# Layer 0 of the context tokens runs in front of the latent tokens, and one latent tile of layer 0 takes gathered experts

## The chip, the cores and the metric

The kernel runs on one core of one Trainium2 chip. The metric is the device time of one execution in microseconds (us): the median of three runs. The profile is one further execution, taken by the hardware profiler. The engines are TensorE (PE, with its weight loads listed as PEld), VectorE (DVE), ScalarE (ACT), GpSimd (POOL) and SyncE (SP). Each runs its own instruction queue in order; SP, ACT and POOL also issue DMA transfers from their queues.

## The reference, cut to what matters

Two layers act on 512 latent tokens x (four tiles of 128) beside 256 context tokens ctx (two tiles). Each layer is: norm, one input projection, differential attention, pooling, short convolution, gates, output projection; then norm and a PEER layer that picks 128 single-neuron experts for each token out of 16384.

```
for l in range(2):
    xn, cn = modulate(rms_norm(h)), modulate(rms_norm(hc))
    k, v of ctx come from cn; ctx attends to ctx alone, x attends to x and ctx
    mix   = mixer_output(attn, pool, conv, gates of xn) @ w_out     # x, both layers
    mix_c = the same of cn                                         # ctx, layer 0 only
    h  = h  + mod[2]  * mix;    h  = h  + mod[5]  * peer_ffn(norm(h))
    hc = hc + mod_c[2]* mix_c;  hc = hc + mod_c[5]* peer_ffn(norm(hc))   # layer 0 only
return h

def peer_ffn(xc):                       # per chunk of 128 tokens
    eidx, gate = product-key top 16 of each of 8 heads   # 128 experts for a token
    hid = gelu(einsum('td,thkd->thk', xc, u_emb[eidx]))
    return einsum('thk,thkd->td', gate * hid, v_emb[eidx])
```

In layer 1 the context gives only its k and v, and its own output is not needed. So the context's layer 0 result is needed late, by layer 1's attention, while x needs the context's layer 0 k and v early.

## The kernel before, in words

Activations lie transposed, channels on partitions and tokens in the free dimension. Every float32 product is made of three float32r matmuls (high times high, high times low, low times high): lines L98, L99 and L100 in `mm3`. A weight tile is loaded raw by SP, and `split` (L93 on ACT, L94 on DVE) makes its high and low half, so each 128x1024 piece costs one ACT and one DVE instruction.

The PEER layer has two forms. **Dense**: all 16384 experts are computed for the tile, and the gates of those not picked are zero. `hidden` runs 128 groups of 24 matmuls (`hid`), `values` 128 groups of 24 (`dps`), with the tokens of all dense tiles as columns: 512 columns for four tiles, 384 for three. `gates` writes the gate matrix, `weigh` multiplies it in. **Gathered**: in `gathered` each token of one tile fetches its own 128 rows of `peer_u` and 128 of `peer_v`; that is 256 indirect DMAs of 128x1024 floats for a tile, issued by POOL (L846) into a ring of three buffers named `row`. Each is consumed by one DVE instruction: L859 (a dot product, for `peer_u`) or L869 (a sum into `gacc`, for `peer_v`). The fetch of a row waits until the DVE instruction three rows back has freed its buffer.

Before, both context tiles of layer 0 and one x tile of layer 1 (`nd = XT - 1`) are gathered: 768 fetches. All four x tiles of layer 0 are dense. Layer 0 projects q, k and v for x and ctx together (`qkv`, one load of each weight for both), attends for both, runs the mixers of ctx and the pooling of x, then `ctx_ffn`, then the other mixers of x, and the x experts. The gathers of ctx are put 40000 behind in priority.

The order of each engine's queue is set when the kernel is built: a tile scheduler with a timeline (`schedule_with_timeline_sim`) places instructions by priority and by the times that it supposes. `prio(shift)` moves the priority of what is written inside. On the chip the queues run in that order whatever the real times are, so a late fetch holds everything that stands behind its consumer on DVE.

Of the kernel before, what the change touches and what calls it, by code (L numbers as in the profile page):

```python
# [21 lines left out]
F32 = mybir.dt.float32  # L22
# [47 lines left out]
class Net:  # L70
# [137 lines left out]
    def rotary(self, l, pool):  # L208
# [4 lines left out]
        nc.sync.dma_start(rows, bass.AP(tensor=r.tensor, offset=r.offset + 384 * l, ap=[[0, P], [1, 2 * HD]]))  # L213
        cs = pool.tile([P, XT, 2, 32], F32, name="cs")
# [10 lines left out]
        gains = [rows[:, off:off + HD] for off in (R_QG, R_KG)]  # L225
# [73 lines left out]
    def qkv(self, l, streams, kinds):  # L299

        nc, a = self.nc, self.a
        with ExitStack() as es:
            ap_ = self.pool(es, f"at{l}{streams[0].i}", 2)
            pm = self.pool(es, f"atm{l}{streams[0].i}", 3, PSUM)
            pt_ = self.pool(es, f"att{l}{streams[0].i}", 2, PSUM)
            rot = self.rotary(l, self.pool(es, f"rot{l}{streams[0].i}"))
# [88 lines left out]
    def attend(self, l, es, parts, side=None):  # L395

        nc = self.nc
        name = f"hd{l}"
# [3 lines left out]
        for s, k0, nk in parts:  # L402
            qs, ks = slice(s.o, s.o + s.n), slice(k0 * P, (k0 + nk) * P)
            for h in range(NH):
# [9 lines left out]
                self.head(l, ap_, pss, pt_, q, k, kl, v, h, s, nk)  # L414

    def head(self, l, ap_, pss, pt_, q, k, kl, v, h, s, nk):
        nc, nq = self.nc, s.nt
        A = []
        for qt in range(nq):
            qc = qt * P  # L420
            at = ap_.tile([P, nk * P], F32, tag="a", name="at", bufs=6)
# [173 lines left out]
    def conv_out(self, l, s, pp, z, m, gates):  # L595

        nc, a = self.nc, self.a
        with ExitStack() as es:
            zp = self.pool(es, f"co{l}{s.i}", 1)
            for c in range(4):  # L600
                g = gates[2 * c:2 * c + 2] if gates else self.conv_gate(l, s, pp, zp, c, 3)
                w = self.load_w(a["conv_out_w"][l, c], KT, 256)
                for cb in range(2):
                    j, t = 2 * c + cb, g[cb]
                    q = zp.tile([P, s.n], F32, tag="cq", name="cq", bufs=3)
                    nc.sync.dma_start(q, self.md[l][j * P:(j + 1) * P, s.o:s.o + s.n])
                    nc.vector.tensor_tensor(t, self.proj_t(pp, self.sub(w, cb), [z])[0][0], t, op=OP.mult)
                    nc.vector.tensor_tensor(t, t, q, op=OP.add)
                    self.split(m.h[:, j], m.l[:, j], t)
# [198 lines left out]
    def values(self, l, n, cs, W, pools, vq, acc, first, last=None):  # L808
# [3 lines left out]
        for dq in range(4):  # L812
# [9 lines left out]
            for db in range(2):  # L822
# [9 lines left out]
                if last is not None:  # L832
                    ht = last.tile([P, n], F32, name="fh", bufs=2)
                    nc.sync.dma_start(ht, self.hmid[l][j * P:(j + 1) * P, 0:n])
                    nc.vector.scalar_tensor_tensor(acc[:, j], acc[:, j], self.modT[l][:, 40 + j, 0:1], ht, op0=OP.mult, op1=OP.add)
                    dst = self.out if l == DEPTH - 1 else self.hout
                    nc.sync.dma_start(dst[j * P:(j + 1) * P, 0:n], acc[:, j])


    def gathered(self, l, tiles, gp, gq, nat, late):  # L840

        nc, a = self.nc, self.a

        def fetch(t, idx, s):
# [367 lines left out]
```

## Time and profile before

| what | us |
|---|---|
| median of three runs | 5145.29 |
| lowest and highest run | 5134.71 and 5170.3 |
| the profiled execution | 5138.01 |
| its span, first to last instruction | 5136.2 |
| PE busy in the span | 4934.7 (96%) |
| DVE busy | 3946.9 (77%) |
| POOL busy | 1180.5 (23%) |
| first matmul of x's dense layer 0 (`hid`) | at 1349.1 |
| first layer 1 matmul of x's norm | at 2986.8 |
| first matmul of the norm in front of layer 1's experts | at 3814.1 |

Matmuls overlap in the pipeline, and the duration of one is longer than its share of time. How fast PE really goes is read from how many matmuls start in a full 100 us, which the window rows below give behind "PE busy" as (x...). The same column of POOL counts the fetches where a window is cut to the tile `row`.

### The profile page before, as it was taken

The numbers are of one execution on the slowest core, as the hardware profiler recorded it, in microseconds if no ns is written. First come the engines' busy times: TensorE is split into PE (matmuls) and PEld (weight loads), VectorE is DVE, ScalarE is ACT, GpSimd is POOL, SyncE is SP. The second block draws the span as 40 slices with busy tenths as digits, with TensorE's granted clock in tenths as the row PEclk, the third lists the DMA queues.
The fourth block names the chain that finished last, engine by engine and source line by source line (L and its number), as shares of the span: only waits on it lengthen the run. The fifth ranks groups of instructions, "written<-read, shape, count | busy, mean of one in ns | idle before, by whom it ended". The sixth has DMA issues, their size and how long they took to land.

```text
span 5136.2 us, 73940 instructions
## 1 busy us (share of the span) xinstructions
PE 4934.7 (96%) x27373; PEld 4195.8 (82%) x27373; DVE 3946.9 (77%) x7993; ACT 1988.4 (39%) x2968; POOL 1180.5 (23%) x1028
## 2 busy tenths in 40 slices
PE   8999999998899999989999999999999999899999
PEld 5688787776688788768888789777679999899999
DVE  5457676697899998568888867666359999787885
ACT  4346664422333344222233234544334344332333
POOL 0001000024433343333333300000000434344320
PEclk9999999999999999999999999999999999999999
DMA  8667453468897889999999845533355888988995
GB/s 305 239 200 224 137 191 108 155 200 273 302 316 259 285 312 339 329 321 326 336 341 344 311 137 166 161 126 97 109 172 174 277 309 331 330 314 294 329 317 177
DMA packets 509035, 1280.77 MB, mean 249 GB/s; under 512 B 42496, under 2 KB 224640, under 8 KB 500352
## 3 DMA queue, kind: packets, MB, share of 16 engines
q1 hardware_dynamic: 302816, 669.35, 38.5%
q0 software_dynamic: 131968, 449.90, 25.7%
q10 hardware_dynamic: 73888, 156.79, 8.1%
q8 instruction: 215, 3.52, 0.3%
q14 instruction: 148, 1.21, 0.1%
HBM read 1098.13 MB, written 177.73 MB: 248 GB/s over the span
## 4 chain that ended last, share of the span: by engine, by line
PE 64%; DMA 14%; DVE 11%; issue 7%; POOL 2%; ACT 1%; SPq 0%; ACTq 0%; POOLq 0%; DVEq 0%
PE mm L98 6%; DMA row<-peer_v,ix 6%; PE mm L100 6%; PE mm L99 6%; DMA row<-peer_u,ix 6%; PE dps L99 5%; PE dps L100 5%; PE dps L98 5%; PE hid L100 4%; PE hid L98 4%; PE hid L99 4%; PE qk L98 3%; PE qk L100 3%; PE qk L99 2%; POOL row L846 2%
## 5 line engine op out<-in xcount | busy, mean ns | idle before, releaser
L100 PE MATMUL hid<-yh,ul 128*128 128x512 f32 (+1 forms) x2048 | 760.2, 372 | 33.9 <-DVE ul L94 33.6
L98 PE MATMUL hid<-yh,uh 128*128 128x512 f32 (+1 forms) x2048 | 757.1, 370 | 21.0 <-ACT yh L286 13.2
L846 POOL DMA_INDIRECT row<-peer_v,ix x384 | 568.5, 1480 | 876.7 <-DVE gacc L869 501.1
L846 POOL DMA_INDIRECT row<-peer_u,ix x384 | 521.4, 1358 | 1059.7 <-DVE row L859 617.7
L99 PE MATMUL hid<-yl,uh 128*128 128x512 f32 (+1 forms) x2048 | 755.7, 369 | 2.3 <-DVE yl L287 2.3
L98 PE MATMUL dps<-wh,vh 128*128 128x512 f32 (+1 forms) x2048 | 735.1, 365 | 20.0 <-ACT vh L93 18.6
L99 PE MATMUL dps<-wl,vh 128*128 128x512 f32 (+1 forms) x2048 | 741.7, 365 | 12.3 <-DVE wl L94 12.3
L100 PE MATMUL dps<-wh,vl 128*128 128x512 f32 (+1 forms) x2048 | 742.0, 364 | 10.4 <-DVE vl L94 10.4
L98 PE MATMUL mm<-hi,whi 128*128 128x512 f32 (+1 forms) x1856 | 666.5, 360 | 12.3 <-DVE y L582 3.1
L100 PE MATMUL mm<-hi,wlo 128*128 128x512 f32 (+1 forms) x1856 | 660.6, 358 | 14.0 <-DVE wlo L94 14.0
L99 PE MATMUL mm<-lo,whi 128*128 128x512 f32 (+1 forms) x1856 | 662.4, 357 | 3.5 <-DVE lo L94 3.5
L859 DVE SCALAR_TENSOR_TENSOR row<-row,gx 128x1024 f32<-128x1024 f32 x384 | 467.0, 1221 | 170.3 <-DMA row<-peer_u,ix 169.5
L869 DVE SCALAR_TENSOR_TENSOR gacc<-row,gw,gacc 128x1024 f32<-128x1024 f32 x381 | 488.1, 1281 | 133.7 <-DMA row<-peer_v,ix 132.6
L94 DVE TENSOR_TENSOR wlo<-wraw,whi 128x1024 fp32r<-128x1024 f32 (+1 forms) x356 | 427.2, 1202 | 179.6 <-ACT whi L93 177.2
L93 ACT ACTIVATE uh<-uraw 128x1024 fp32r<-128x1024 f32 x256 | 271.5, 1061 | 716.4 <-PE hid L99 651.9
L93 ACT ACTIVATE whi<-wraw 128x1024 fp32r<-128x1024 f32 (+1 forms) x356 | 370.5, 1043 | 404.4 <-PE mm L99 305.2
L93 ACT ACTIVATE vh<-vraw 128x1024 fp32r<-128x1024 f32 x256 | 270.2, 1058 | 641.9 <-PE dps L99 395.1
L100 PEld LDWEIGHTS hid<-yh,ul 128*128 128x128 f32 x2048 | 390.2, 191 | 82.9 <-DVE ul L94 44.6
L98 PEld LDWEIGHTS hid<-yh,uh 128*128 128x128 f32 x2048 | 391.1, 191 | 64.1 <-ACT yh L286 15.6
L98 PEld LDWEIGHTS dps<-wh,vh 128*128 128x128 f32 x2048 | 386.7, 189 | 61.9 <-ACT vh L93 19.4
L99 PEld LDWEIGHTS dps<-wl,vh 128*128 128x128 f32 x2048 | 387.1, 189 | 54.8 <-DVE wl L94 14.4
L100 PEld LDWEIGHTS dps<-wh,vl 128*128 128x128 f32 x2048 | 387.2, 189 | 51.5 <-DVE vl L94 11.1
(332 smaller groups left out, 9480.4 us busy)
## 6 DMA issues: line engine op xcount, KB each, us to landing
uraw<-uT SPq DMA_DIRECT2D x256, 512.0 KB, 5.7
vraw<-v SPq DMA_DIRECT2D x256, 512.0 KB, 6.8
wraw<-w_in SPq DMA_DIRECT2D x216, 512.0 KB, 4.4
gd<-gst ACTq DMA_DIRECT2D x28, 2048.0 KB, 10.7
mw<-w_mod SPq DMA_DIRECT2D x96, 512.0 KB, 7.0
wraw<-wq SPq DMA_DIRECT2D x80, 512.0 KB, 6.0
hidd<-ge ACTq DMA_DIRECT2D x128, 256.0 KB, 5.6
G<-gd SPq DMA_DIRECT2D x32, 1024.0 KB, 10.7
```

The lines of the kernel that those rows point to most:

```text
L93: self.nc.scalar.activation(hi, src, AF.Copy)
L94: self.nc.vector.tensor_tensor(lo, src, hi.bitcast(F32), op=OP.subtract)
L98: mm(ps, lh, rh, start=start, stop=False)
L99: mm(ps, lh, rl, start=False, stop=False)
L100: mm(ps, ll, rh, start=False, stop=stop)
L846: nc.gpsimd.indirect_dma_start(out=r, out_offset=None, in_=a[t], in_offset=bass.IndirectOffsetOnAxis(ap=idx[:, s:s + 1], axis=0))
L859: nc.vector.scalar_tensor_tensor(out=r, in0=r, scalar=1.0, in1=x, op0=OP.mult, op1=OP.mult, accum_out=hid[:, k:k + 1])
L869: nc.vector.scalar_tensor_tensor(acc, r, w[:, k:k + 1], acc, op0=OP.mult, op1=OP.add)
```

## The change

Layer 0 is written as `trunk0`, layer 1 as `trunk1`. In `trunk0` the norm, q, k, v, attention, mixers and `ctx_ffn` of ctx come first, and x's q, k, v, attention and mixers after them, with a second load of the 12 weights of q, k and v. The weights of layer 1's modulation move from the start to x's projection. In layer 0 now one x tile (`gath = (1, 1)`) is gathered and three are dense; its fetches have a priority of 1000 + 28 for each row before it, those of ctx stay at 40000. The gather pools of ctx and of x are separate, each with its own ring of three `row` buffers. A layer 0 gather ends by writing its sum to DRAM (`natc`, `natx`); `gather_end` reads it back, transposes it and adds it to the residual: for x at the end of layer 0, for ctx in layer 1 behind x's projections, pooling and convolution ("pca"), with a second load of the 8 weights of k and v. Layer 1's x attention is issued behind that.

```diff
-    def trunk(self, l, X, Cx, ges, eh, h):
+    def trunk0(self, X, Cx):
...
+        ges, gpools = self.gather_pools("c0")
...
+            self.load_norm(0, Cx, load(Cx), lambda: self.modulation(0, (0,), mp, pp))
+            self.load_norm(0, X, load(X), side="right")
+            with self.prio(500):
+                self.modulation(0, (1, 2), mp, pp)
...
+        self.qkv(0, [Cx], "kqv")
+        with ExitStack() as ea, ExitStack() as e2:
+            self.attend(0, ea, [(Cx, XT, CT)], "right")
+            hc = self.mixers(0, Cx, self.pool(e2, "fc", 2, PSUM), cp, "pckvgo")
+        self.ctx_ffn(0, hc, gpools)
+        ec.close()
+        with ExitStack() as e2:
+            mp, pp = self.pool(e2, "mod1"), self.pool(e2, "mod1p", 2, PSUM)
+            self.modulation(1, (0, 1, 2), mp, pp)
+            self.qkv(0, [X], "kqv", "right")
+        with ExitStack() as ea, ExitStack() as e2:
+            self.attend(0, ea, [(X, 0, TT)], "right", 1)
+            hm = self.mixers(0, X, self.pool(e2, "fl0", 2, PSUM), xp, "pc|kvgo", ea)
         return ges, e3, hm
 
+    def trunk1(self, X, Cx, ges, eh, h):
...
+        self.norm(1, X, h, self.a1, 0, "a10", side="right")
+        eh.close()
+        self.qkv(1, [X], "kqv")
+
+        def begin():
+            ges.close()
+            with ExitStack() as ec:
+                self.parts(ec, "xc1", Cx)
+                self.load_norm(1, Cx, lambda h, hp, es: self.gather_end(0, self.natc, NX, NC, 1, hp, self.pool(es, "gq", 1, PSUM), h))
+                self.qkv(1, [Cx], "kv")
+            self.attend(1, ea, [(X, 0, TT)], "right")
+
+        with ExitStack() as e2:
+            hm = self.mixers(1, X, self.pool(e2, "fl1", 2, PSUM), xp, "pcakv|go", ea, begin)
+        return e3, hm
...
+        self.gath, self.late = (1, 1), ((1000, 28), (40000, 0))
...
-        nd = XT if l == 0 else XT - 1
+        nd = XT - self.gath[l]
...
+        n = 0
+        for h in range(8):
+            hid = gp.tile([P, 16], F32, name="ghid", bufs=2)
+            for k in range(16):
+                with self.prio(late[0] + n * late[1]):
+                    r = fetch("peer_u", h * 16 + k)
+                    nc.vector.scalar_tensor_tensor(out=r, in0=r, scalar=1.0, in1=x, op0=OP.mult, op1=OP.mult,
+                                                   accum_out=hid[:, k:k + 1])
+                n += 1
...
+        if end is None:
+            with self.prio(late[0] + n * late[1]):
+                nc.sync.dma_start(nat, acc)
...
+    def gather_end(self, l, nat, c, n, i, gp, gq, h):
+
+        nc = self.nc
+        nc.sync.dma_start(h, self.hmid[l][:, c:c + n].rearrange("(k p) t -> p k t", p=P))
+        for t in range(n // P):
+            acc = gp.tile([P, D], F32, tag="gend", name="gend", bufs=1)
+            nc.sync.dma_start(acc, nat[t * P:(t + 1) * P, :])
+            self.gather_add(l, acc, i, gq, h[:, :, t * P:(t + 1) * P])
...
+            if nd < XT:
+                self.gather_end(l, self.natx[l], n, NX - n, 0, vf, vq, acc[:, :, n:])
+                nc.sync.dma_start(self.hout[:, n:NX].rearrange("(k p) t -> p k t", p=P), acc[:, :, n:])
```

What moves on the queues is shown at three places. The first is POOL during x's attention of layer 0. In these rows `hk`, `hq`, `hkl` and `hv` are the five loads of one attention head, `row` is one fetch of the gather, and the number behind `ix` tells whose list of experts it takes (6329 and 7244: the two ctx tiles, 16079: the x tile). Before, the loads of a head follow one another:

```order
L408 DMA hk<-kd_65 128x1536
L406 DMA hq<-qd_63 128x2x512
L410 DMA hkl<-ld_67 128x768
L413 DMA hv_5116<-vd_69 128x768
L413 DMA hv_5117<-vd_69 128x768
```

After the change the same loads stand between the fetches of the first ctx tile:

```order
L850 DMA row<-peer_v,ix_6329 128x1024 x11
L850 DMA row<-peer_u,ix_6329 128x1024 x4
L415 DMA hv_10930<-vd_69 128x768
L415 DMA hv_10931<-vd_69 128x768
L850 DMA row<-peer_u,ix_6329 128x1024
L410 DMA hk<-kd_65 128x1536
L850 DMA row<-peer_u,ix_6329 128x1024
L408 DMA hq<-qd_63 128x2x512
L412 DMA hkl<-ld_67 128x768
L850 DMA row<-peer_u,ix_6329 128x1024 x10
```

So the loads of a head, and the small memsets of pooling and convolution, now wait in line behind fetches, which wait for their buffers. Before, no fetch stood on POOL until x's attention was over.

The second place is POOL in layer 0's x experts. Before, the two ctx lists follow one another whole, out of one ring (10999 is the first):

```order
L846 DMA row<-peer_u,ix_10999 128x1024 x16
L846 DMA row<-peer_v,ix_10999 128x1024 x6
L1019 IOTA rank 128x2048
L846 DMA row<-peer_v,ix_10999 128x1024 x10
L846 DMA row<-peer_u,ix_10999 128x1024 x16
```

After:

```order
L850 DMA row<-peer_u,ix_7244 128x1024 x3
L850 DMA row<-peer_u,ix_16079 128x1024 x3
L850 DMA row<-peer_u,ix_7244 128x1024
L850 DMA row<-peer_v,ix_7244 128x1024 x2
L850 DMA row<-peer_u,ix_16079 128x1024 x3
L850 DMA row<-peer_v,ix_7244 128x1024
```

The second ctx tile and the x tile alternate from the 391st fetch to the 640th, so that two rings of three buffers are in use there; the 128 fetches behind that are the x tile's alone.

The third place is DVE at the end of layer 0, where `acc<-dps` adds a dense group, `row,ghid` and `gacc` consume fetches, `gtr` is the gathered sum after its transpose, and `nrm<-nps` begins layer 1's norm of x. Before:

```order
L831 TENSOR_TENSOR acc<-dps,acc 128x512
L835 SCALAR_TENSOR_TENSOR acc<-acc,modT_98,fh 128x512
L875 SCALAR_TENSOR_TENSOR gres<-gtr,modT_98,gres 128x128 x2
L94 TENSOR_TENSOR wlo<-wraw,whi 128x1024 x3
L123 TENSOR_SCALAR nrm<-nps 128x512
```

After:

```order
L836 TENSOR_TENSOR acc<-dps,acc 128x384
L865 SCALAR_TENSOR_TENSOR row,ghid<-row,gx 128x1024
L840 SCALAR_TENSOR_TENSOR acc<-acc,modT_99,fh 128x384
L865 SCALAR_TENSOR_TENSOR row,ghid<-row,gx 128x1024
L94 TENSOR_TENSOR wlo<-wraw,whi 128x1024
L865 SCALAR_TENSOR_TENSOR row,ghid<-row,gx 128x1024
L94 TENSOR_TENSOR wlo<-wraw,whi 128x1024 x2
L865 SCALAR_TENSOR_TENSOR row,ghid<-row,gx 128x1024 x10
L871 TENSOR_TENSOR gw<-gw,gk_16080 128x16
L878 SCALAR_TENSOR_TENSOR gacc<-row,gw,gacc 128x1024 x16
L900 SCALAR_TENSOR_TENSOR acc<-gtr,modT_99,acc 128x128 x8
L123 TENSOR_SCALAR nrm<-nps 128x512
```

Before, the last fetch of layer 0 is consumed ahead of the last dense groups. After, 29 fetches of the x tile follow the last dense group, and layer 1's norm of x waits for them.

## Rows read from the trace of the kernel before

**Rows 1.** The page, part 1: busy time, share of the span, instructions.
```profile
PE 4934.7 (96%) x27373; PEld 4195.8 (82%) x27373; DVE 3946.9 (77%) x7993; ACT 1988.4 (39%) x2968; POOL 1180.5 (23%) x1028
```
**Rows 2.** Stages by windows (start:end, length, busy and count by engine, clock, DMA).
```profile
core 0: us, PE busy (x) PEld busy (x) DVE busy (x) ACT busy (x) POOL busy (x), PEclk, DMA share, GB/s
0.00:100.00 100.00, 84.01 (x450) 42.83 (x450) 51.77 (x155) 41.97 (x69) 2.20 (x9) 0.97 0.81 298
500.00:600.00 100.00, 95.41 (x569) 73.79 (x568) 76.05 (x151) 59.28 (x100) 6.90 (x19) 0.98 0.50 162
...
1083.00:1349.00 266.00, 228.74 (x936) 177.50 (x935) 203.79 (x272) 71.69 (x90) 118.34 (x101) 0.96 0.83 283
1400.00:1500.00 100.00, 99.31 (x611) 88.88 (x609) 91.91 (x270) 34.80 (x47) 33.31 (x32) 1.00 0.93 326
1500.00:1600.00 100.00, 97.49 (x527) 84.11 (x527) 98.99 (x364) 34.96 (x48) 23.32 (x24) 0.98 0.81 266
...
2500.00:2600.00 100.00, 100.00 (x443) 82.84 (x442) 88.77 (x121) 29.68 (x37) 41.64 (x28) 1.00 0.96 338
2700.00:2800.00 100.00, 100.00 (x443) 82.84 (x442) 87.78 (x117) 29.21 (x37) 34.41 (x30) 1.00 0.99 348
2987.00:3814.00 827.00, 807.01 (x4186) 645.51 (x4184) 513.36 (x1035) 358.82 (x538) 27.57 (x82) 0.98 0.42 134
3100.00:3200.00 100.00, 100.00 (x863) 100.00 (x863) 69.37 (x200) 43.52 (x63) 0.00 (x0) 1.00 0.49 161
3814.00:5136.00 1322.00, 1258.36 (x7841) 1232.43 (x7841) 1111.78 (x2223) 494.41 (x735) 393.26 (x257) 0.98 0.81 284
4300.00:4400.00 100.00, 100.00 (x775) 95.18 (x775) 95.33 (x126) 47.28 (x79) 47.10 (x24) 1.00 0.93 347
5000.00:5100.00 100.00, 100.00 (x580) 99.93 (x579) 64.50 (x100) 35.50 (x49) 0.00 (x0) 1.00 0.62 210
```
**Rows 3.** The same windows for the tile `row` alone; POOL's count is the fetches.
```profile
1200.00:1300.00 100.00, 43.14 (x55) 43.21 (x35) 0.95 0.81 276
1400.00:1500.00 100.00, 38.76 (x46) 33.31 (x32) 1.00 0.93 326
1500.00:1600.00 100.00, 30.11 (x36) 23.32 (x24) 0.98 0.81 266
1600.00:1700.00 100.00, 36.24 (x45) 38.87 (x30) 0.98 0.79 261
...
4500.00:4600.00 100.00, 40.08 (x48) 43.22 (x33) 0.98 0.90 316
```
**Rows 4.** The instructions on the tile `row`; start of the first fetch; landing times.
```profile
L846 POOL DMA_INDIRECT row<-peer_u,ix x384: 932/1145/5817, 1083.6 to 4889.2; - x192
...
DMA to landing us min/median/max: 4.1/6.8/14.8
```
**Rows 5.** Timeline of DVE in the dense gather (start, us, instruction, idle before).
```profile
1213.79 1.22 DVE L859 SCALAR_TENSOR_TENSOR row<-row,gx 128x1024 f32<-128x1024 f32 x1
1214.93 0.09 DVE L859 DVE_READ_ACCUMULATOR row<-row,gx 128x1 f32 x1
1214.93 1.22 DVE L94 TENSOR_TENSOR wlo<-wraw,whi 128x1024 fp32r<-128x1024 f32 x1
...
1223.07 1.23 DVE L859 SCALAR_TENSOR_TENSOR row<-row,gx 128x1024 f32<-128x1024 f32 x1 [1.95 <-DMA row<-peer_u,ix]
```
**Rows 6.** Timeline of POOL, the fetch that the last row above consumes.
```profile
1215.29 1.68 POOL L846 DMA_INDIRECT row<-peer_u,ix  x1 [0.60 <-DVE row L859]
```
**Rows 7.** Groups by line and form: count, busy us, mean ns.
```profile
L751 PE MATMUL gps<-gB,gA 128*128 128x128 f16 x1792 | 128.5, 220 | 4.4 <-DVE gB L743 4.2
...
L94 DVE TENSOR_TENSOR wl<-gel,wh 128x512 fp32r<-128x512 f32 x128 | 83.8, 686 | 0.1
...
L94 DVE TENSOR_TENSOR wl<-gel,wh 128x384 fp32r<-128x384 f32 x80 | 41.3, 553 | 3.0 <-ACT wh L93 3.0
```
**Rows 8.** The chain of waits at the end of layer 0 (start, us, what).
```profile
2929.95 8.04 DMA row<-peer_v,ix
...
2986.80 1.72 PE nps L275 x4
```

More of the change, by code (lines that the diff above doesn't have):

```diff
@@ L213, in rotary @@
         nc.sync.dma_start(rows, bass.AP(tensor=r.tensor, offset=r.offset + 384 * l, ap=[[0, P], [1, 2 * HD]]))
+        gains = [rows[:, off:off + HD] for off in (R_QG, R_KG)]
+        if not turn:
+            return None, None, gains
         cs = pool.tile([P, XT, 2, 32], F32, name="cs")
@@ L879, in load_norm @@
-    def load_norm(self, l, s, hsrc, between=None, side=None):
+        with self.prio(late[0]):
+            x = gp.tile([P, D], F32, name="gx", bufs=1)
+            nc.sync.dma_start(x, nat)
+            acc = gp.tile([P, D], F32, name="gacc", bufs=1)
+        n = 0
[7 more added lines that the diff above has]
+                n += 1
+            w = gp.tile([P, 16], F32, name="gw", bufs=2)
+            with self.prio(late[0] + n * late[1]):
+                nc.scalar.activation(w, hid, AF.Gelu_apprx_tanh)
+                nc.vector.tensor_tensor(w, w, g[:, h * 16:h * 16 + 16], op=OP.mult)
+            for k in range(16):
+                with self.prio(late[0] + n * late[1]):
+                    r = fetch("peer_v", h * 16 + k)
+                    if h == 0 and k == 0:
+                        nc.vector.tensor_scalar(acc, r, w[:, k:k + 1], None, op0=OP.mult)
+                    else:
+                        nc.vector.scalar_tensor_tensor(acc, r, w[:, k:k + 1], acc, op0=OP.mult, op1=OP.add)
+                n += 1
@@ L880, in load_norm, with gather_add @@
+    def gather_add(self, l, acc, i, gq, h):
+        tr = gq.tile([P, 4, P], F32, tag="gtr", name="gtr", bufs=1)
+        for k in range(KT):
+            self.nc.tensor.transpose(tr[:, k % 4], acc[:, k * P:(k + 1) * P], self.ident)
+            self.nc.vector.scalar_tensor_tensor(h[:, k], tr[:, k % 4], self.modT[l][:, 40 + k, i:i + 1], h[:, k], op0=OP.mult, op1=OP.add)
+    def load_norm(self, l, s, load, between=None, side=None):
         with ExitStack() as es:
@@ L973, in mixers @@
+    def mixers(self, l, s, pp, xp, order, attn=None, begin=None):
         z, m, gates = Stream(s.o, s.n, s.i), Stream(s.o, s.n, s.i), []
@@ L1013, in gather, with gather_out @@
         nc.vector.tensor_copy(gk, g)
-        dst = self.hout if l == 0 else self.out
-        self.gathered(l, [(rows, ix, gk, self.hmid[l][:, cols], i, dst[:, cols])], gp, gq, self.natd[l], late)
+        self.gathered(nat, ix, gk, gp, late, end)
+    def gather_out(self, gp, gq, acc, c):
+        col = lambda d: d[:, c].rearrange("(k p) t -> p k t", p=P)
+        h = gp.tile([P, KT, P], F32, tag="row", name="gres", bufs=3)
+        self.nc.sync.dma_start(h, col(self.hmid[DEPTH - 1]))
+        self.gather_add(DEPTH - 1, acc, 0, gq, h)
+        self.nc.sync.dma_start(col(self.out), h)
     def ranks(self, mp):
```

223 lines of the change are left out of this document (86 added, 137 removed).

## The prediction

> **What bounds the kernel now.** I read the page's busy shares first: PE is at 96%, DVE at 77%, POOL at 23% [rows 1]. A busy PE is not a PE at its pace, so the windows come next, for how many matmuls start in 100 us. Where nothing holds PE, 443 matmuls of 512 columns start (0.2257 us each), 580 of 384 columns (0.1724 us) and 863 of 256 (0.1159 us) [rows 2]. Against these paces the values stage of layer 0 loses nothing, although 28 fetches stand in each 100 us. But from 1083 to 1349, where x's mixers run beside a dense gather, 936 matmuls start in 266 us, 211 us of PE at its pace: a fifth is lost while the page calls PE busy.
>
> What holds it there is the gather. Only 35 fetches start in 100 us [rows 3], with DMA at 276 GB/s and not full. The timelines show why: the DVE instruction that frees a buffer ends at 1215.01, POOL starts the next fetch into it at 1215.29, its row is consumed at 1223.07, after DVE had sat idle for it, and freed at 1224.30: 9.3 us for one of three buffers [rows 5, 6]. 35 in 100 us are 2.86 us a fetch, 8.6 us a buffer. Beside the experts it was 33, so 3.0 us [rows 3]. DVE takes the rows in its written order, so what stands behind a late row is late too. So I price the change by counting, along the written order of DVE, how many fetches stand in each stretch, against the work of PE and DVE in it.
>
> **The change, part by part.** PE: layer 0's 3072 `hid` and 3072 `dps` matmuls go from 512 to 384 columns: 6144 x (0.2257 - 0.1724) = 327 us less. If columns alone counted it would be a quarter, 6144 x 0.0564 = 347. The Trainium skill's "Perfetto Trace Analysis" (Optimizing Tensor Performance, Matmuls) says that larger matmuls are more efficient; the trace agrees, by the 20 us between the two. 256 of the 1792 gate matmuls fall away as well; all of them kept PE busy for 128.5 us [rows 7], so 18. Together 345.
>
> DVE: in the dense timeline instructions follow 1.14 us after one another where each lasts 1.22 [rows 5], so about 1.17 us for a fetch's consumer and 1.14 for a weight half. 256 fetches more are 300 us; 40 weight pieces loaded a second time are 46; 64 gate products and 376 smaller tiles (0.13 us less each [rows 7]) give back 38 and 50. DVE gains 258 us: from 3947 to 4205, on a kernel that is to be 345 shorter on PE. SP loads 40 pieces more (21 MB, hidden: DMA is far from full where they fall). ACT does 40 splits more and fewer evictions, and it is at 39%.
>
> So layer 0 now holds 768 fetches where 512 stood, and it ends when the last x row is in. By stretches:
>
> 1. The ctx front, to the first fetch. Its matmuls at their pace are 399 us by count (2688 of 256 columns are 312). Nothing of x fills the waits, the first 41 MB take 137 us at the 298 GB/s of the start [rows 2], the norm and the top-16 stand alone. Ends: 399, and 530 if PE goes at three quarters of its pace as beside attention before (569 matmuls in the window at 500, 66 us if all were of 256 columns, a little more with the wider ones [rows 2]). I take 485: DVE's work there, some 400, is as large as PE's.
> 2. x's projection, 38 fetches, PE 207: 215. x's attention with pooling and convolution, 81 fetches, PE 222, DVE 245. In the attention window before DVE got to 76% [rows 2], at the most 98%: 250 to 322. I take 275.
> 3. From the middle of the attention to x's output projection, 194 fetches beside 255 us of PE. At 2.86 us they take 555; with half the weight traffic beside them a row may land a little sooner than the 7.7 us of the example; the quickest of all landed in 4.1 [rows 4], which would make 5.7 us a buffer, 369. I take 2.7: 525. **Here 270 us of PE's time go.**
> 4. The keys, 89 fetches, PE 276, DVE 310. In the same stage before, 86 fetches took 300 us with DVE at 91 to 99% [rows 2, 3]: 315.
> 5. Rest of the keys, gates, `hid`, and the first values, 258 fetches, PE 607. Two rings alternate, so the single ring's wait is gone for most of it; at 3.0 us it would be 780. But now DMA is full: 135 MB of fetched rows, 44 of `uT`, 27 of `v`, 25 of gate matrix written and 13 read, 16 of `hidd` written and 13 read, 3 of other weights: 276 MB, at the 345 GB/s that the chip did at most [rows 2] 800 us. DVE's work is 707. I take 798.
> 6. The values after that, 79 fetches, PE 319: 325.
> 7. The tail: 29 fetches behind the last dense group, with nothing else on DVE: 2.7 us each, 78. Then the sum goes to DRAM and back, 12. PE stands idle.
>
> Sum: 485 + 215 + 275 + 525 + 315 + 798 + 325 + 78 + 12 = 3028, where layer 1's norm of x began at 2987 before [rows 8].
>
> Layer 1 to its experts took 827 before [rows 2]. Its PE work stays. ctx's norm and second projection move behind x's convolution; x's attention then has less beside it, 10 us more by the idle of the attention windows. `natc` was written hundreds of us earlier, so its reading waits for nothing. 837. The experts of layer 1 are untouched: 1322 [rows 2].
>
> 3028 + 837 + 1322 = 5187, and 1.8 around the span: **5190 us**, against 5138 for the profiled execution. That execution stands 0.14% under the median of 5145, so I forecast no change, leaning to slower: the 345 us that PE saves are spent on waiting for rows.
>
> **Rivals.** The gathers keep up. If landing is much quicker without dense work beside it (the 4.1 us [rows 4]) then stretch 3 goes to 370, stretch 5 to PE's 607 with DVE's 707 on top, and PE sets layer 0: 5138 - 345, plus 75 for a front without cover, is 4870. For it speaks the values stage, where 28 fetches in 100 us cost PE nothing [rows 2]; against it the window of 266 us, where they did, and DMA at 0.96 to 0.99 share with 28 or 30 fetches [rows 2]. The Trainium skill's "DMA: Bandwidth & Descriptors" (Anatomy of one DMA, SWDGE path) gives 2.0 us plus bytes over 436 GB/s for such a transfer, an estimate of 3.2 us for a row tile of 524288 bytes, and by that the gathers would keep up; the trace does not agree, with 4.1 us at the least and 6.8 in the middle [rows 4]. Chance 0.23.
>
> Slower: POOL's line. In x's attention the five loads of a head and pooling's memsets stand behind up to 15 fetches. If a head's loads come later than the one head of lead that two buffers give, some 35 us, attention waits for POOL, DVE for attention, and the fetches for DVE: a ring that feeds on itself. It decides once 12 fetches (12 x 2.86) lie in front of a load; the order has such places. Then stretch 2 costs its 322 and 3 goes at the 3.0 to 3.1 of the experts, 600: 122 us more, 5310. Chance 0.27.
>
> The forecast keeps 0.50, with 5110 to 5270 for itself. That the change doesn't happen is excluded by the order of the queues.
>
> **The numbers.** 1% is about what a measurement of this kernel can tell from no change, so within 1% is 5094 to 5197. Of the forecast's 0.50, 0.30 is within, 0.17 slower, 0.03 faster; of the first rival's 0.23, 0.20 faster, 0.03 within; of the second's 0.27, 0.25 slower, 0.02 within. Faster 0.23, within 0.35, slower 0.42. The range reaches from 5050, which leaves out most of the first rival, to 5310, the second.
>
> **What would show it.** Right: layer 1's norm of x starts between 2960 and 3110; from x's attention to its output projection about 33 to 38 fetches in 100 us and DVE idle for `row`; DMA at 0.95 or more in the gates; a hole on PE of 70 to 100 us at the end of layer 0. Wrong: over 45 fetches in 100 us with one ring; a first fetch before 420 or after 540; a layer 1 front more than 40 us from 837; or PE at 580 matmuls in 100 us through layer 0's experts, which would be the first rival.

## The result, and the profile after

The changed kernel takes 5458.5 us (median of four runs, 5442.0 to 5459.9) against 5144.5 for the kernel before beside it: 1.0595 times as long, 95% interval 1.0551 to 1.0638. I had forecast 5190, in a range to 5310. The page of the changed kernel answers to [rows 1]:

```profile
PE 4848.0 (89%) x27130; PEld 4228.5 (78%) x27130; DVE 4200.2 (77%) x8370; ACT 1968.6 (36%) x2971; POOL 1467.7 (27%) x1284
```

DVE's work is what I had summed (4205). PE has lost the work it was to lose, by count and shape: all 6144 matmuls of layer 0's `hid` and `dps` have 384 columns, and 1536 gate matmuls are left of 1792. Its busy time fell by 87 us only, at a mean granted clock of 0.91 where it had been 0.98. And 608 us of the span now have no matmul at all, against 202 before. The windows of the changed kernel, with the columns of [rows 2], show where:

```profile
100.00:200.00 100.00, 89.68 (x564) 72.11 (x564) 61.65 (x181) 45.89 (x83) 13.27 (x40) 0.89 0.70 217
400.00:500.00 100.00, 77.40 (x473) 64.94 (x472) 50.74 (x107) 43.79 (x79) 0.00 (x0) 0.83 0.49 158
550.00:650.00 100.00, 58.28 (x354) 52.07 (x355) 87.34 (x373) 17.62 (x25) 22.69 (x18) 0.73 0.51 178
1200.00:1300.00 100.00, 74.96 (x156) 39.44 (x154) 81.41 (x143) 29.01 (x52) 46.49 (x49) 0.50 0.78 247
1300.00:1400.00 100.00, 57.24 (x125) 31.59 (x125) 77.16 (x120) 21.07 (x37) 43.88 (x42) 0.50 0.75 231
1660.00:3175.00 1515.00, 1300.29 (x7843) 1251.81 (x7841) 1351.36 (x2533) 509.42 (x748) 645.28 (x459) 0.93 0.93 333
2000.00:2700.00 700.00, 595.22 (x3603) 560.56 (x3602) 641.28 (x1073) 237.94 (x368) 368.73 (x237) 0.93 0.96 355
3175.00:4124.00 949.00, 890.80 (x4199) 688.12 (x4200) 539.29 (x1065) 351.31 (x532) 27.41 (x82) 0.87 0.38 123
3738.00:4000.00 262.00, 238.31 (x622) 139.98 (x623) 141.48 (x289) 87.27 (x165) 15.78 (x36) 0.62 0.25 77
4124.00:5455.00 1331.00, 1262.13 (x7849) 1234.73 (x7847) 1113.10 (x2224) 497.59 (x738) 369.21 (x257) 0.98 0.81 282
```

There are two poor places besides the front. In layer 0, 156 and 125 matmuls start in 100 us while the last heads of x's attention run (1200 to 1400); in layer 1, 622 start in the 262 us of x's attention. Where nothing holds PE it is 443 of 512 columns in 100 us. In both PE was granted about half its clock, 0.50 and 0.62 (0.50 is the lower level, 1.2 GHz). It stood idle for 68 of the 200 us in layer 0, but for only 24 of the 262 in layer 1: there, at the low clock, the heads' own matmuls nearly fill it. The fetches, with the columns of [rows 3] (DVE, POOL, clock, DMA share, GB/s), and the tile's instructions and landing times, as in [rows 4]:

```profile
1142.00:1669.00 527.00, 242.84 (x290) 220.48 (x194) 0.71 0.81 268
1660.00:3175.00 1515.00, 568.92 (x683) 641.82 (x457) 0.93 0.93 333
2700.00:3000.00 300.00, 88.03 (x109) 88.12 (x71) 1.00 0.97 341
```

```profile
L850 POOL DMA_INDIRECT row<-peer_u,ix x512: 935/1082/5828, 600.5 to 5207.0; - x171
...
DMA to landing us min/median/max: 4.1/7.0/14.9
```

From the middle of x's attention to its output projection 194 fetches took 527 us, 36.8 in 100 us. The end of layer 0, in the chain of waits (start, us, what), answers to [rows 8]:

```profile
3161.32 4.88 DMA row<-peer_v,ix
3166.29 1.29 DVE gacc L878
3167.60 2.62 DMA natx<-gacc
3170.24 3.18 DMA gend<-natx
3175.05 2.08 PE nps L277 x2
```

Counting what DVE has consumed gives the end of each of my stretches:

| stretch, by rows consumed | forecast, us | measured, us |
|---|---|---|
| ctx front, to the first row | 485 | 606 |
| x's projection, to row 38 | 215 | 249 |
| x's attention, first half, to 119 | 275 | 287 |
| to x's output projection, 313 | 525 | 527 |
| keys, 402 | 315 | 324 |
| rest of the keys, gates, `hid`, first values, 660 | 798 | 784 |
| values, 739 | 325 | 317 |
| tail, 768, and sum through DRAM | 78 + 12 | 72 + 9 |
| layer 1 from norm to norm | 837 | 949 |
| layer 1's experts | 1322 | 1332 |

All fetch-bound terms held within 14 us. Two terms carry the miss of 268: the front (121, and 34 behind it) and layer 1's front (112). Two of my signs of a wrong forecast are there: the first fetch starts at 600.5, past 540, and layer 1's front is more than 40 us from 837. One of a right forecast is missing: layer 1's norm of x starts at 3175, past 3110.

### The profile page after: what moved, and what is told of

Its sections match the earlier page's. It is cut to its first block, busy times and chain, and to the rows that moved or that the text cites. A ratio compares the mean times of both kernels' runs of the same rounds, so it can differ in the third digit from the quotient of the medians.

```text
span 5455.9 us, 74522 instructions
## 1 busy us (share of the span) xinstructions
PE 4848.0 (89%) x27130; PEld 4228.5 (78%) x27130; DVE 4200.2 (77%) x8370; ACT 1968.6 (36%) x2971; POOL 1467.7 (27%) x1284
## 4 chain that ended last, share of the span: by engine, by line
PE 53%; DVE 14%; DMA 14%; issue 12%; POOL 4%; ACT 3%; ACTq 0%; SPq 0%; POOLq 0%; DVEq 0%
PE mm L98 6%; PE mm L99 6%; PE mm L100 6%; DMA row<-peer_v,ix 6%; DMA row<-peer_u,ix 4%; POOL row L850 4%; PE dps L100 4%; PE dps L99 3%; PE dps L98 3%; PE hid L100 3%; PE hid L98 3%; PE hid L99 3%; DVE row L865 2%; DVE gacc L878 2%; PE qk L99 2%
## 5 line engine op out<-in xcount | busy, mean ns | idle before, releaser
L100 PE MATMUL hid<-yh,ul 128*128 128x384 f32 x2048 | 711.1, 349 | 60.5 <-DVE ul L94 60.2
L865 DVE SCALAR_TENSOR_TENSOR row<-row,gx 128x1024 f32<-128x1024 f32 x512 | 620.7, 1217 | 185.2 <-DMA row<-peer_u,ix 184.7
L98 PE MATMUL hid<-yh,uh 128*128 128x384 f32 x2048 | 711.0, 348 | 51.4 <-ACT uh L93 32.1
L878 DVE SCALAR_TENSOR_TENSOR gacc<-row,gw,gacc 128x1024 f32<-128x1024 f32 x508 | 647.1, 1278 | 121.7 <-DMA row<-peer_v,ix 120.5
L98 PE MATMUL dps<-wh,vh 128*128 128x384 f32 x2048 | 685.9, 339 | 34.2 <-ACT vh L93 22.4
L99 PE MATMUL hid<-yl,uh 128*128 128x384 f32 x2048 | 704.1, 344 | 0.7 <-DVE yl L289 0.7
L99 PE MATMUL dps<-wl,vh 128*128 128x384 f32 x2048 | 688.5, 338 | 10.8 <-DVE wl L94 10.8
L100 PE MATMUL dps<-wh,vl 128*128 128x384 f32 x2048 | 675.0, 339 | 21.9 <-DVE vl L94 21.6
L98 PEld LDWEIGHTS mm<-hi,whi 128*128 128x128 f32 x1856 | 361.9, 195 | 124.1 <-ACT hi L93 53.5
L100 PEld LDWEIGHTS mm<-hi,wlo 128*128 128x128 f32 x1856 | 361.0, 194 | 65.5 <-DVE wlo L94 17.0
```

The lines of the kernel that those rows point to most:

```text
L98: mm(ps, lh, rh, start=start, stop=False)
L99: mm(ps, lh, rl, start=False, stop=False)
L100: mm(ps, ll, rh, start=False, stop=stop)
L865: nc.vector.scalar_tensor_tensor(out=r, in0=r, scalar=1.0, in1=x, op0=OP.mult, op1=OP.mult, accum_out=hid[:, k:k + 1])
L878: nc.vector.scalar_tensor_tensor(acc, r, w[:, k:k + 1], acc, op0=OP.mult, op1=OP.add)
```

## The experiments

Each kernel is the changed one with one edit, if nothing else is said. Ratios are to the kernel before, with 95% intervals; "front of layer 1" is from its first norm to the norm of its experts. Those experts, whose work no edit changes, took from 1324 us (all3) to 1357 (l1_warm) in the profiles, for a reason that no run settles. So a difference of up to 30 us between two kernels need not come from the edit, and the stages are read beside the times.

**Layer 1's order.** First the attention ahead of pooling and convolution:

```diff
-            hm = self.mixers(1, X, ..., "pcakv|go", ea, begin)
+            hm = self.mixers(1, X, ..., "apckv|go", ea, begin)
```

> The changed kernel, but in layer 1 the context's end, its second projection and x's attention are issued ahead of x's pooling and convolution and not behind them. Theory (bunching): layer 1's front took 945 us where I had 837, because x's attention stood behind the dense work and had only the convolution gates and their output beside it; its eight heads took 264 us with PE mostly empty. Then the heads spread again to about 50 us each, with pooling and convolution between them, the front of layer 1 falls to 830 to 860 us and the time to about 5350 us (5330 to 5380). Rival (the context's second projection and the reading of its sums are what costs): the front stays within 25 us of 945, and the time is 5435 to 5480.

Measured: 5410.7 us (1.0512; 1.0494 to 1.0529), the front 887. Half of the gain came. The heads did spread, to some 52 us each, but a new loss came ahead of them. The window around it, and PE's longest waits there (line, releaser: us, times, longest):

```profile
3280.00:3440.00 160.00, 127.36 (x979) 120.12 (x978) 104.82 (x272) 62.42 (x96) 4.25 (x8) 0.87 0.54 173
```

```profile
PE gtr L899 <- DMA gend<-natc: 14.1, 2, 10.7
PE tr L382 <- DVE zz L370: 7.2, 1, 7.2
```

The context's end stood alone there. With the context's end and the attention between pooling and convolution:

```diff
-            hm = self.mixers(1, X, ..., "pcakv|go", ea, begin)
+            hm = self.mixers(1, X, ..., "packv|go", ea, begin)
```

> The changed kernel, but in layer 1 the context's end, its second projection and x's attention are issued behind x's pooling and ahead of its convolution. With the attention ahead of both, the heads spread to 52 us each, but the front of layer 1 came down by 48 us only, since PE lost some 60 us around x's projection while the context's end was read, normed and projected. Theory (both are one thing: a chain of small steps needs dense work that may run beside it): pooling now covers the context's end and convolution and gates the attention; the front goes from 945 to about 845 us, the time to 5340 to 5375. Rival (the context's end has a price of its own that no cover removes, some 50 us): 5395 to 5420, as with the attention first.

Measured: 5420.3 us (1.0534; 1.0510 to 1.0558), the front 914; the wait for `natc` stayed, and at the end of the attention cover (dense matmuls that can run between a head's steps) ran out again. The rival's number, but its cause is not settled by this run. The next one settles it: the order as before, with the context's end first and one projection of both.

```diff
-        self.qkv(1, [X], "kqv")
-        def begin(): ...      # ctx end, its k and v, attend; called in "pcakv|go"
+        ges.close()
+        self.load_norm(1, Cx, lambda h, hp, es: self.gather_end(...))
+        self.qkv(1, [X, Cx], "kqv")
+        self.attend(1, ea, [(X, 0, TT)], "right")
+        hm = self.mixers(1, X, ..., "pckv|go", ea)
```

> The changed kernel with layer 1's order undone: the context's end and norm directly behind x's norm, q, k and v of x and ctx in one projection with one load of the weights, x's attention issued ahead of pooling, convolution and gates, as before. Layer 0 stays as changed. Theory (the front of layer 1 is long because of what stands beside the two chains of small steps): the front, 949 us from norm to norm, goes to 830 to 850, and the time to 5340 to 5365. Rival (the context's end, taken from DRAM and transposed, has a price of its own, as with the attention first or in the middle, which gave 887 and 914): 870 to 910, and 5385 to 5420.

Measured: 5355.9 us (1.0407; 1.0375 to 1.0439), the front 834. Its windows:

```profile
3177.00:4011.00 834.00, 802.61 (x4199) 643.08 (x4200) 514.31 (x1056) 354.47 (x531) 25.84 (x82) 0.97 0.39 128
3460.00:3860.00 400.00, 400.00 (x1706) 300.06 (x1706) 252.66 (x440) 187.56 (x286) 17.54 (x56) 1.00 0.33 105
```

The same 4199 matmuls take 115 us less; 1706 start in 400 us of attention where 622 started in 262, at the full clock. So layer 1's order, with the second projection of the context that belongs to it, costs 103 us of the 314. With a joint projection the context's end costs next to nothing: the front is 834, where it was 827 before.

Is the low clock a cause there? Behind each score of layer 1's attention:

```diff
+                if l:
+                    w = self.warm.tile([P, 512], F32, tag="mm", name="warm")
+                    for _ in range(4):
+                        nc.tensor.matmul(w, self.X.h[:, 0, :P], self.X.h[:, 1], start=True, stop=True)
```

> The changed kernel with 4 matmuls of 512 columns, whose result nobody reads, behind each score of layer 1's attention: 256 of them, 58 us of PE at its pace, between the steps of the heads, where PE was granted 0.55 of its clock and DVE waited 65 us in all for scores. Theory (the low clock lengthens the heads' chain): the granted clock there rises to 0.9 or more, heads come to under 31 us each, and the time stays within 15 us of 5458 or falls, though work was added. Rival (the chain over DVE and ACT sets the heads, whatever the clock): the heads stay at 34 us or get longer by the added matmuls, and the time rises by 20 to 60 us.

Measured: 5502.5 us (1.0692; 1.0658 to 1.0725). But the added matmuls did not stay between the heads' steps. In the order as built all 256 start ahead of the stretch in which the 0.62 was read; the second line is that stretch in this run:

```profile
L436 PE MATMUL warm<-hi x256: 387/393/504, 3589.6 to 3718.5; 128*128 128x512 f32 x128
3738.00:4020.00 282.00, 261.88 (x859) 170.37 (x858) 152.15 (x291) 112.62 (x188) 13.94 (x33) 0.78 0.29 92
```

Dense work stands there in their place: two heads have 213 and 208 matmuls in 50 and 51 us, at the full clock, and the later ones are as bare as before. So the rise from 0.62 to 0.78 is not the doing of matmuls between the steps, and the run doesn't answer its question. Of the 45 us that its profile is longer, 20 lie in the front of layer 1 and 25 in the experts behind it.

Other rows answer it in part. A head is 74 matmuls of its own. Here are three that had next to nothing beside them, from one head's end to the next, two of the changed kernel and one of l1_mid:

```profile
3834.00:3871.00 37.00, 34.40 (x77) 19.30 (x76) 18.97 (x41) 11.73 (x24) 2.98 (x6) 0.50 0.25 75
3871.00:3903.00 32.00, 28.93 (x75) 16.06 (x74) 19.58 (x42) 11.53 (x23) 2.70 (x6) 0.66 0.29 87
3912.00:3939.00 27.00, 23.17 (x70) 13.12 (x69) 18.22 (x40) 11.49 (x23) 1.44 (x11) 0.78 0.32 96
```

And here is where a score's four matmuls begin and where the next matmul follows, without idle time between, in the changed kernel at the full clock and at half of it:

```profile
3766.09 0.50 PE L429 MATMUL sc<-hk,hq 128*128 128x512 f32 x1 [0.38 <-ACT p L438]
3767.58 0.50 PE L99 MATMUL po<-tl,hv 128*128 128x512 f32 x1
3850.55 0.80 PE L429 MATMUL sc<-hk,hq 128*128 128x512 f32 x1
3853.02 0.79 PE L99 MATMUL po<-tl,hv 128*128 128x512 f32 x1
```

1.49 us against 2.47 for the same work. So the low clock does lengthen a bare head, by some 10 us between 0.78 and 0.50, and PE is idle for under 4 us of each. What a bare head takes at the full clock is left open. The cure that worked was useful work beside the heads, and with it the clock was back at 1.00 (l1_old).

**The two parts alone.** All four x tiles dense in layer 0, in the new order:

```diff
-        self.gath, self.late = (1, 1), ((1000, 28), (40000, 0))
+        self.gath, self.late = (0, 1), ((1000, 28), (40000, 0))
```

> The changed kernel with all four x tiles of layer 0 dense, so that the new order stands alone. Theory (the gathered tile pays, the order costs): PE gets 345 us back to do, the tail of 80 us in front of layer 1 goes, the gates and the first values are no longer full of fetches; layer 0 ends at about 3340 and the time is 5560 to 5640 us. Rival (the 256 added fetches cost more than the 345 us of PE they save): 5470 us or less.

Measured: 5589.7 us (1.0864; 1.0846 to 1.0882). And the gathered tile in the old order: the kernel before with the edits of the experts alone,

```diff
-        nd = XT if l == 0 else XT - 1
+        nd = XT - 1
-                    ... self.gather(l, pools, ep, ..., 40000)
+                    ... self.gather(l, pools, ep, ..., (40000, 0) if l else (1000, 28), self.natx[l])
+            nc.sync.dma_start(acc[:, :, n:], self.hout[:, n:NX].rearrange("(k p) t -> p k t", p=P))
```

> The kernel before with one gathered x tile in layer 0, fetched out of a ring of its own as in the change, so that the gathered tile stands alone in the old order. Theory (fetches need the early start that the new order gives them): the first fetch is at about 1090 as before; some 140 fetches until x's list is known, 3.1 to 3.6 us for each after that, so some 250 to 300 fetches are left when the dense work is done at 2650, and layer 0 ends at 3050 to 3250; 5200 to 5400 us in all. Rival (the old order would have carried the gathered tile): two rings together reach 2 us a fetch, PE sets layer 0's end at about 2700 to 2800, and the time is 4850 to 4960 us.

Measured: 5391.1 us (1.0479; 1.0458 to 1.0500). So the gathered tile gains 131 us in the new order and costs 248 in the old one; the new order costs 446 us with four dense tiles and 67 with three. In the old order 173 rows were still out when the dense work was done, and PE stood (timeline: start, us, instruction, idle before):

```profile
2855.00:3215.00 360.00, 5.02 (x14) 2.08 (x12) 230.80 (x278) 4.25 (x8) 187.50 (x173) 0.50 0.80 268
```

```profile
3206.95 0.47 PE L881 MATMUL gtr<-ident,gacc 128*128 128x128 f32 x1 [351.19 <-DVE gacc L875]
```

**What rows cost.** Without the fetches of the context:

```diff
+        if late[0] == 40000 and end is None:
+            ...   # gacc set to zero and written to nat
+            return
```

> The changed kernel without the 512 fetches of the context's experts and their sums; zeros are written in their place, so this leaves out part of the computation. Theory (in layer 0 waiting rows hold DVE's line, and with it the attention): x's attention, which took 49 us or more a head, comes to about 35 us a head, x's keys start at 1370 to 1470 and not at 1669, and the time is about 5000 us (4900 to 5080). Rival (the attention has too little dense work beside it, whether rows are fetched or not): heads stay at 45 us or more, keys start later than 1550, and the time falls by less than 250 us.

Measured: 5059.6 us, one run. x's experts begin at 1453 and not at 1660, and take 1295 us and not 1515; the last heads of layer 0 take 27 to 33 us each, the first ones about 60, and the front loses what it lost (3541 matmuls in its first 606 us, 3528 in the changed kernel). The theory's time and start came, its heads only in part: rows cost the trunk some 207 us and the experts 220. The window of the experts, all and for `row` alone:

```profile
1453.00:2748.00 1295.00, 1249.48 (x7846) 1222.90 (x7844) 1110.87 (x2225) 502.76 (x739) 358.50 (x257) 0.99 0.88 305
```

```profile
1453.00:2748.00 1295.00, 318.50 (x384) 356.96 (x256) 0.99 0.88 305
```

One buffer more for the context's rows:

```diff
-            r = gp.tile([P, D], F32, tag="row", name="row", bufs=3)
+            r = gp.tile([P, D], F32, tag="row", name="row", bufs=nb)   # 4 for ctx, 3 for x
-        ot = ap_.tile([P, nq * P], F32, tag="ot", name="ot", bufs=2)
+        ot = ap_.tile([P, nq * P], F32, tag="ot", name="ot", bufs=1)
```

> The changed kernel with four row buffers in place of three for the context's gather (and one buffer less for the attention's output, to make room). Theory (one of three buffers comes round in 8.6 us, and that sets the fetches beside x's attention and mixers): a fetch there comes to 2.2 to 2.4 us, x's experts' norm starts 80 to 150 us earlier than 1660, part of which is given back where DMA is full; the time is 5340 to 5420. Rival (rows land later when more are under way, or DVE's own work sets the pace): the norm starts within 40 us of 1660 and the time is 5430 to 5480.

Measured: 5405.7 us (1.0512; 1.0479 to 1.0545). Rows 119 to 313 came in 470 us and not 527, 2.42 us each, about the 2.4 of the ring theory. But x's experts' norm came at 1669, no earlier. In x's attention, from 855 to 1414, DVE was busy for 483 of 559 us (464 in the changed kernel), PE was again at 0.50 of its clock from 1200 to 1400, and the last head ended 27 us later, at 1422; which of the two held the heads is not shown. The gain appears later, since fewer rows were left for the experts, which took 1450 us:

```profile
1669.00:3119.00 1450.00, 514.94 (x618) 605.44 (x410) 0.95 0.93 332
```

Five and four buffers in the old order with the gathered tile:

```diff
-            r = gp.tile([P, D], F32, tag="row", name="row", bufs=3)
+            r = gp.tile([P, D], F32, tag="row", name="row", bufs=nb)   # layer 0: 5 for ctx, 4 for x
```

> The old order with the gathered x tile, as in old_order, but five row buffers for the context and four for x in place of three and three. There 684 rows were left for x's experts, which took 1876 us, 350 of them with PE empty. Theory (a row waits for its turn in the ring): rows come by a third to two thirds faster, the experts fall to PE's 1310 plus some tail, 1450 to 1600, and the time to 5000 to 5130. Rival (DMA is full: 684 rows and the dense weights, gates and hidden values are some 590 MB, 1720 us at 345 GB/s): the experts stay at 1720 or more, and the time at 5230 to 5320.

Measured: 5227.7 us (1.0178; 1.0161 to 1.0195); x's experts took 1715 us, 5 us under the rival's bound:

```profile
1350.00:3065.00 1715.00, 1398.97 (x7866) 1334.56 (x7865) 1565.05 (x2827) 510.15 (x752) 913.78 (x639) 0.89 0.94 349
2000.00:2900.00 900.00, 686.07 (x3548) 654.76 (x3547) 816.63 (x1132) 231.26 (x335) 551.43 (x400) 0.86 1.01 379
```

The 350 us hole is gone, but DMA is full for 900 us, and PE starts 3548 matmuls in them where 5220 of 384 columns would fit. With three dense tiles the experts' length follows the rows left for them:

| kernel | rows left | x's experts, us |
|---|---|---|
| no_ctx | 256 | 1295 |
| ring_c4 | 410 | 1450 |
| changed kernel | 457 | 1515 |
| front_b (below) | 525 | 1587 |
| old_order, three buffers | 683 | 1876 |
| old_ring, five and four | 637 | 1715 |

That is 1.1 us a row on average from 256 to 525; with three buffers in the old order it is 1.8 from there to 683. With four dense tiles 208 rows (l0_dense, 1654 us) and 426 (before, 1660) cost the same: PE has 345 us more to do there, and the rows hide beneath it.

**The front.** x's projection ahead of the context's experts, at a lower priority:

```diff
+        with self.prio(3000):
+            self.qkv(0, [X], "kqv", "right")
         self.ctx_ffn(0, hc, gpools)
...
-            self.qkv(0, [X], "kqv", "right")
```

> The changed kernel with x's projection issued ahead of the context's experts (at a lower priority, by 3000) and not behind them, so that it can fill the context's output projection, norm, keys and lists. Theory (missing cover): the windows from 400 to 650, which lost some 110 us, lose half of that; the first fetch stays within 60 us of 606, x's keys start 30 to 70 us earlier than 1669, and the time is 5390 to 5430. Rival (the front's chain of small steps on DVE sets it, cover or not): x's projection pushes the context's steps back by what it gains, 5445 to 5500.

Measured: 5459.6 us (1.0606; 1.0578 to 1.0635), the rival's time, though x's experts began at 1579, 81 us earlier; DVE took the first row at 768. By stages layer 0 and the front of layer 1 are 16 us shorter together, and layer 1's experts took 1354 us and not 1332. One projection of both, as before:

```diff
-        self.qkv(0, [Cx], "kqv")
+        self.qkv(0, [X, Cx], "kqv")
...
-            self.qkv(0, [X], "kqv", "right")
```

> The changed kernel, but with one projection of x and ctx together in front of the context's attention, as before, and one load of its weights; all else of the new order stays. So x's projection stands beside the front of ctx and no longer behind it. Theory (what went wrong in the front is missing cover: 200 us lost to the first fetch where I had 86): the same work loses some 60 us less, the first fetch comes at 740 to 780, and as x's 215 us of projection no longer follow, the time falls to 5400 to 5440 us. Rival (layer 0 lives by the start of its fetches): they start 150 us later, nothing behind them gets shorter, and the time rises to 5500 or more.

Measured: 5422.1 us (1.0535; 1.0510 to 1.0561). The first row came at 741, x's experts began at 1574, 86 us earlier. But the experts took 72 us longer:

```profile
0.00:741.00 741.00, 656.30 (x4681) 566.35 (x4681) 487.41 (x1488) 329.71 (x552) 42.90 (x107) 0.93 0.58 190
741.00:1574.00 833.00, 703.15 (x2561) 463.98 (x2561) 604.97 (x936) 249.53 (x369) 320.94 (x312) 0.85 0.76 260
1574.00:3161.00 1587.00, 1326.38 (x7844) 1268.43 (x7842) 1428.82 (x2636) 512.27 (x750) 758.21 (x527) 0.93 0.94 341
```

Both expectations were half right: cover was missing in the front, and giving it leaves 525 rows for the experts and not 457. Layer 0 ended at 3175, 3162 and 3161 in the three kernels, wherever x's projection stood.

**Together, and two designs.** The edits of l1_old, front_b and ring_c4 in one kernel:

> The changed kernel with three of the edits together: layer 1 in the old order, four row buffers for the context's gather, and one projection of x and ctx in layer 0. Alone they gave 102, 53 and 36 us. If they are three separate losses, they add: 191 us less, 5260 to 5280. If the ring and the projection are the same rows counted twice (both decide how many rows are left for the experts, and pull in opposite directions there), the two together give 53 to 60: 5295 to 5310.

Measured: 5250.3 us (1.0218; 1.0202 to 1.0233), 208 us less than the changed kernel where the three alone sum to 191, and 10 us under the range for that. So they are not the same rows counted twice; why they give more than their sum is left open.

The last 128 rows of the context moved into layer 1, with layer 0 in the old order and layer 1's as in l1_mid (`rest` issues the last four of the eight blocks of rows):

```diff
+        self.rest(self.pool(er, "late1", 1, side="right"), 6)
         self.qkv(1, [X], "kqv")
```

> A design from what the runs showed: layer 0 in the order of the kernel before, with one gathered x tile out of a ring of its own, but the last 128 rows of the second ctx tile are fetched in layer 1, beside x's projection and pooling, out of a ring of six buffers; the context's end and x's attention stand behind x's pooling, ahead of its convolution. In the old order with the gathered tile PE stood still from 2900 to 3250, waiting for the last fetches. Theory (layer 0 is short of time for fetches, layer 1's front has room): the hole falls to under 80 us, layer 0 ends at 2900 to 2980, layer 1's front takes 850 to 920, and the time is 5080 to 5220 us. Rival (rows in layer 1's front hold DVE's line there as they did in layer 0): the front takes 1000 us or more, and the time is over 5280.

Measured: 5408.3 us (1.0514; 1.0485 to 1.0543); layer 0 ended at 3006, after a hole of 78 us and not 350, as the theory had it, but the front of layer 1 took 1062. The rival held: rows delay DVE's q and k steps, for which PE waits. Its window, and PE's longest wait in it:

```profile
3006.00:3400.00 394.00, 267.65 (x1659) 242.50 (x1659) 321.06 (x617) 111.62 (x161) 161.88 (x146) 0.83 0.74 264
```

```profile
PE qk L98 <- DVE qy L346: 98.3, 11, 17.7
```

The kernel before with six buffers in layer 0's gather:

```diff
-            r = gp.tile([P, D], F32, tag="row", name="row", bufs=3)
+            r = gp.tile([P, D], F32, tag="row", name="row", bufs=nb)   # 6 in layer 0
```

> The kernel before with six row buffers in place of three in layer 0's gather, and nothing else. Theory (the ring held PE only from 1083 to 1349, beside x's mixers, where a fifth of PE's pace was lost, 55 us): half of that comes back, 15 to 35 us, 5108 to 5130. Rival (DVE's own work held PE there, or DMA): within 10 us of before's 5143.

Measured: 5169.4 us (1.0055; 1.0041 to 1.0069), a little slower. From 1083 to 1349 PE started 1147 matmuls, 936 before [rows 2]. But the written order changed too, DVE took the first row 28 us earlier (1064, not 1092), and the 83 us ahead of that window started 213 matmuls. Before they had 409, by the window of the kernel before:

```profile
1000.00:1083.00 83.00, 83.00 (x409) 68.12 (x408) 77.86 (x327) 23.87 (x32) 2.39 (x9) 1.00 0.34 114
```

Over both windows that is 1360 against 1345, so the loss moved to the front, and that the ring held PE there, as I had read it, is not shown. Layer 0 ended 17 us later (3004, not 2987), and layer 1's experts took 23 us more. What six buffers alone are worth is left open. None of the kernels that compute the whole is shorter than the one before.

## Why the prediction was wrong

**PE -345, DVE +258.** Right as a count of work; DVE's sum came out 5 us from the measured one. The sums go by PE's pace at the full clock, though, and have no term for a lower one.

**Stretch 1, the front: 485, at most 530.** Mis-sized: 606. The count of PE's work was sound, but my pace was not. I took the upper end from an attention window in which x's matmuls stood between the steps. Alone, the context's matmuls went at two thirds of their pace, 399 in 606, and the windows show it: from 400 to 500 PE starts 473 matmuls while DMA's share is 0.49 and DVE is busy for 51 of 100, so nothing is full there, and steps wait for each other; from 550 to 650 it starts 354, and DVE, with the lists of experts, is busy for 87. PE's granted clock is 0.83 and 0.73 in the two; how much of the loss that makes, no run separates. front_a and front_b show that x's projection covers the front: x's experts begin 81 and 86 us earlier. front_b also shows a second fault in the step, that an earlier or later front shifts the end one to one. With rows still to be fetched it doesn't: 72 of the 86 came back in the experts.

**Stretches 2 to 7.** Right in sum: 2320 us measured from row 38 on, with the sum through DRAM, for 2328 forecast. The sign of DMA full in the gates came (0.96 share, 355 GB/s; my 345 was low as the most before, [rows 2] have 348), the hole of PE at the end was 80 us, by PE's wait for `natx`:

```profile
PE gtr L899 <- DMA gend<-natx: 80.4, 1, 80.4
```

Why stretch 3 came out right is a little different from what I wrote. ring_c4 shows that the ring did set the rows' pace, but not the end of the stretch: with faster rows the heads end later, and the gain shows in the experts.

**Layer 1 to its experts: 837.** This step failed, and its mechanism with it: I wrote that x's attention "then has less beside it, 10 us more by the idle of the attention windows". Those windows were of attention *with* pooling, convolution and gates beside it, and their idle time says nothing on what an attention costs that has only the gates and the convolution's output beside it. It took 112 us more than forecast, and l1_old gives 115 of them back by the order with its joint projection. What the runs show in place of those 10 us: in the 262 us of the window 531 of the 622 matmuls are the heads' own, and the other 91, of 512 columns, are 21 us by the pace in [rows 2]. So the heads stood nearly bare, PE's clock fell to 0.62, and at that clock the same matmuls take longer, 37 us for a head at 0.50 and 27 at 0.78. With cover (l1_old) PE was full at 1.00. Counting the dense matmuls left beside the heads would have told that cover runs out, but no row that I had read prices it.

**Rival: the gathers keep up.** Wrong: 36.8 rows in 100 us, landing in 7.0 us in the middle. The Trainium skill's "DMA: Bandwidth & Descriptors" (Anatomy of one DMA, SWDGE path) would give an estimate of 3.2 us for such a transfer; this trace doesn't agree either.

**Rival: POOL's line, slower.** The sign was right, the mechanism wrong. In the last 300 us of x's attention of layer 0, from 1100 to 1400, PE's waits (line, releaser: us, times, longest) name no load of a head. The longest:

```profile
PE sc L429 <- ACT p L438: 28.8, 14, 5.7
PE po L99 <- DVE tl L94: 28.3, 14, 4.4
PE po L98 <- ACT th L93: 15.4, 22, 0.7
PE tr L450 <- DVE at L445: 12.2, 3, 6.2
```

PE waits for steps on ACT and DVE; the loads behind 15 fetches were in time.

**What stays open.** How much of the front's loss is which step, and how much the clock; what the heads would take at the full clock without cover; what a deeper ring is worth in the kernel before; why layer 1's experts differ by 33 us between kernels.

## What to carry to other kernels

What a chain of small steps (an attention head, a norm, a list of experts) costs depends on the dense work issued beside it, so when an order is changed, count for each chain the matmuls that are left to stand between its steps; idle time read where cover was ample does not price the chain without it, and the granted clock has to be read beside it. Moving work from a full engine to rows fetched by DMA pays only while the rows fit under what PE still has to do: here each row from 256 to 525 in the experts' stage made it longer by 1.1 us on average. And a gain at the front of a stage that ends on a shared resource has to be followed to the end of that stage before it is counted.

## What the runs showed of the hardware

With more buffers in flight DMA moved more than the most I had seen before: 379 GB/s over 900 us of rows and weights (old_ring), where I had taken 345 as the limit. PE can be nearly busy and at half its clock at once: attention heads without dense work beside them took 37 us at a granted clock of 0.50, 32 at 0.66 and 27 at 0.78, and the four matmuls of a score, one behind the other, 2.47 us at 0.50 and 1.49 at 1.00.
